# One encoder layer on one core: the scan's within-chunk products of a group run together, B-by-C products in pairs, transposes may be held back longer

## The chip, the core and the metric

The kernel runs on one core of a Trainium2 chip. The metric is the device time of one execution in microseconds (us); of the kernel before it is 1085.19 us, the median of 3 runs from 1084.91 to 1087.61. The engines are TensorE (PE in the profile; its weight loads are PEld), VectorE (DVE), ScalarE (ACT), GpSimd (POOL) and SyncE (SP, which issues the DMAs).

## The reference

One layer of a bidirectional hybrid encoder: 512 tokens, 1024 channels, everything float32.

```python
h = rmsnorm(x, pre_mix_norm)
z, xbc, dt_raw, q, k, v, gates = split_cols(h @ w_in, IN_SPLITS)     # 1024 x 10816
y_ssd  = ssd_branch(z, xbc, dt_raw, ...)                             # 32 heads of 64, 8 groups, state 128, chunk 128
y_attn = window_attention(q, k, v, sink, rel_table) @ w_attn_out     # 16 heads, 4 kv heads, +-128 tokens
g = sigmoid(gates + b_gate)
x = x + rmsnorm((g_ssd * y_ssd + g_attn * y_attn) @ w_o, post_mix_norm)
x = x + rmsnorm(square(relu(rmsnorm(x, pre_mlp_norm) @ w_mlp_in)) @ w_mlp_out, post_mlp_norm)
```

The change lies in `ssd_branch`, whose core is a scan in chunks of 128 tokens, run once forward and once on the flipped sequence, the two results added:

```python
cb = einsum('bclgn,bcsgn->bcgls', c, b)                               # B by C in a chunk, one per group
y_diag = einsum('bcgls,bcgrls,bcsgrp->bclgrp', cb, decay, xdt)        # within a chunk
states = einsum('bclgn,bcgrl,bclgrp->bcgrpn', b, decay_states, xdt)
y_off = einsum('bclgn,bcgrpn,bcgrl->bclgrp', c, prev, exp(a_cs))      # from the chunks before
u = (y_fwd + y_bwd + xs * d_skip) * silu(z)
u = u * rsqrt(mean(u * u over the group) + EPS) * norm_w
```

## The kernel before

**Products.** The large products take both operands in two parts, a rounded one and the remainder (`wh` and `wl` for weights, `hi` and `lo` or names ending in `h` and `l` for activations), and sum three products of 512 columns per block of 128 inputs (`mm3`, through `mm` at L398). They are the *wide* products here. The weights come by DMA as `wr`, ScalarE rounds them to `wh` (L473), GpSimd or VectorE forms `wl` (L477), in rings of three buffers. The small products of scan and attention are plain float32 (`mm`), and so are transposes by the identity (`tr`, L402).

**The scan.** The input projection runs in quanta (one block of 128 output columns over all 512 tokens: 24 wide products). For each of 8 groups (4 heads, 256 channels) `ssd_steps` gives closures that are placed between quanta:

- `prep(c)`, once for each of the 4 chunks: B by C (two records on PE), masked for both directions on VectorE (`cb`, L1103), then `m`, the within-chunk weights of the 4 heads (L1104 to L1115).
- `states0`, `states1`: the state that enters each chunk (`pv`).
- `outs(j)`, once for each pair of chunks (1, 0) and (2, 3): `C` by `pv`, the four heads' products of `m` with `x`, then the sums: the state part times the decay `E` (L1143), the within-chunk part added to `w` (L1144, VectorE), `E` added (L1148, GpSimd), the gate `z` (L1149), squares (`sq`, ScalarE) and their sum `ssq` (L1156); after the second pair `ssq` is split in `sh` and `sl`.
- `rms`, `finish`: PE sums the squares over channels (`ps<-sh,ones_r` and `sl`), the root is taken by way of two DMAs, and the scaled result `yT` is kept and later split (`split_y`, L1233 and L1234). The output projection (`ssd_out_quanta`) uses the last two blocks, of group 7, in its step `rest`.

The products of `m` with `x` write 64 output partitions each and go in pairs to the two halves of the array's columns; so do the attention's products of `pT` with `V`. I call them *half-width*; each leaves two records in the profile, of 128 columns. A *stretch* is a run of half-width products with nothing else between; a *visit* is a run of anything small between wide products.

**What sets the order.** The code emits instructions in program order with its placements; `Planner` then orders each engine's instructions by itself, and the program is built in this order. The planner assigns each instruction a cost (`duration`) and PE a cost of changing between kinds (`change`); a *kind* is whether the operands are the rounded type, and whether the product is half-width. On PE, `next_matmul` takes the first ready instruction in program order, but stays with the present wide kind until another has been ready for `HOLD = 4000` ns; from a small kind it goes on with the same kind, then with any other small one. The other engines take the instruction that is due first. `depend` collects what each instruction waits for; `turn` says that an instruction may start only once another has started, for a buffer that is used in a ring.

## Time and profile before

| | |
|---|---|
| median of 3 runs | 1085.19 us (1084.91 to 1087.61) |
| the profiled execution | 1085.44 us |
| its span, first to last instruction | 1083.7 us |
| mean granted clock of TensorE | 0.997 |
| busy: PE, POOL, DVE, ACT | 1073.5, 808.1, 785.1, 654.4 us |

The span holds, in order: the start (to about 60 us), input projection, scan and attention (to about 619), the scan's output projection (to about 705), the mixing product and the MLP. The 8 groups' scans lie between about 118 and 640 us, a group every 53 us or so in the later part. A line of the timeline gives start, length, engine, source line, operation, output<-inputs by the program's names, shape and count; in brackets the idle time of the engine before it and what ended it. A line of the groups ends in count, busy us, mean ns, and idle time before.

### The profile page before, as it was taken

Reading aid. Unit: us, or ns where it says so; the run is one execution under the profiler, and the core shown is the slowest. Engines: PE = TensorE matmul, PEld = TensorE weight load, DVE = VectorE, ACT = ScalarE, POOL = GpSimd, SP = SyncE. Lnnn points to the kernel's source line nnn. Section 1 sums busy time; section 2 is a strip of 40 time slices with the busy share of each in tenths; the row PEclk is TensorE's granted clock in tenths of the full one; section 3 lists DMA queues with packets and bytes.
Section 4 is the critical chain, followed back from the end, with each engine's and each line's share of the span. In section 5 each row is a group of like instructions: output and inputs, shape, how many; then the busy total and the mean of one; then the engine's idle time right before and its main releaser. Section 6 shows DMA issues by size and latency. Waiting matters only on the chain.

```text
span 1083.7 us, 16956 instructions
## 1 busy us (share of the span) xinstructions
PE 1073.5 (99%) x5584; PEld 902.2 (83%) x5584; DVE 785.1 (72%) x1345; ACT 654.4 (60%) x1407; POOL 808.1 (75%) x1011
## 2 busy tenths in 40 slices
PE   9999999999999999999999999999999999999997
PEld 8888888888888888888888888889888888888885
DVE  6578787788796787887877558668873755755787
ACT  5566776686865767676686522476755434434443
POOL 4446567557558898989898768566998978978844
PEclk9999999999999999999999999999999999999999
DMA  7444624625536555556564389754722612611522
GB/s 218 118 121 125 150 76 123 146 74 158 131 107 164 149 144 160 158 143 167 136 179 113 103 253 332 226 198 127 237 65 59 201 53 59 198 55 59 161 93 78
DMA packets 221000, 152.21 MB, mean 140 GB/s; under 512 B 12493, under 2 KB 194229, under 8 KB 220912
## 3 DMA queue, kind: packets, MB, share of 16 engines
q1 hardware_dynamic: 220764, 151.06, 48.6%
q8 instruction: 44, 0.72, 0.3%
q14 instruction: 44, 0.36, 0.1%
q10 hardware_dynamic: 148, 0.07, 0.0%
HBM read 138.19 MB, written 12.91 MB: 139 GB/s over the span
## 4 chain that ended last, share of the span: by engine, by line
PE 94%; DVE 2%; DMA 2%; ACT 1%; SPq 1%; issue 1%; POOL 0%; POOLq 0%; DVEq 0%
PE pp L398 66%; PE ps L398 25%; PE ps L402 3%; DMA x<-in_x 1%; DMA wr<-in_w_in 0%; ACT b L423 0%; DVE B L944 0%; DVE x L1401 0%; DVE P L855 0%; DVE x L1655 0%; DVE acc L1621 0%; SPq L383 0%; SPq L570 0%; DVE Q L832 0%; DVE ag L1648 0%
## 5 line engine op out<-in xcount | busy, mean ns | idle before, releaser
L398 PE MATMUL pp<-b,wh 128*128 128x512 f32 (+1 forms) x1840 | 564.8, 388 | 0.2 <-DVE b L424 0.2
L477 POOL TENSOR_TENSOR wl<-wr,wh 128x256 fp32r<-128x256 f32 (+1 forms) x503 | 418.2, 860 | 137.4 <-ACT wh L473 133.9
L398 PEld LDWEIGHTS pp<-b,wh 128*128 128x128 f32 x1840 | 340.2, 188 | 68.2 <-issue 1.5
L398 PE MATMUL pp<-b,wl 128*128 128x512 f32 (+1 forms) x920 | 356.5, 388 | 0.0
L398 PEld LDWEIGHTS pp<-b,wl 128*128 128x128 f32 x920 | 172.9, 188 | 34.3
L473 ACT CAST wh<-wr 128x1024 fp32r<-128x1024 f32 x131 | 136.5, 1042 | 82.0 <-PE pp L398 56.1
L1575 POOL TENSOR_TENSOR wl<-wd,wh 128x256 fp32r<-128x256 f32 x168 | 139.8, 862 | 39.9 <-ACT wh L1571 31.9
L1571 ACT CAST wh<-wd 128x512 fp32r<-128x512 f32 x108 | 63.2, 618 | 53.9 <-PE pp L398 23.8
L398 PE MATMUL ps<-wh,fh 128*128 128x512 f32 (+1 forms) x196 | 75.5, 385 | 0.5 <-DVE acc L1621 0.5
L398 PE MATMUL ps<-wl,fh 128*128 128x512 f32 (+1 forms) x196 | 75.5, 385 | 0.0
L398 PE MATMUL ps<-wh,fl 128*128 128x512 f32 (+1 forms) x196 | 75.4, 385 | 0.0
L1112 ACT ACTIVATE n<-cb,tables 128x128 f32<-128x128 f32 x128 | 48.8, 391 | 26.8 <-DVE cb L1103 22.8
L1449 DVE SCALAR_TENSOR_TENSOR pp<-pp,r 128x512 f32<-128x512 f32 (+1 forms) x31 | 17.5, 565 | 54.0 <-ACT r L1446 53.9
L1575 POOL TENSOR_TENSOR wl<-wt,wh 128x256 fp32r<-128x256 f32 x56 | 45.4, 844 | 9.9 <-ACT wh L1571 6.0
L944 DVE SCALAR_TENSOR_TENSOR u<-pp,cv,u 128x510 f32<-128x510 f32 (+1 forms) x64 | 47.6, 744 | 2.9 <-ACT u L940 1.7
L1042 POOL TENSOR_TENSOR xd<-x,tables 128x256 f32<-128x256 f32 x48 | 35.0, 747 | 19.5 <-ACT x L967 16.9
L1113 ACT ACTIVATE m<-cb,tables 128x128 f32<-128x128 f32 x128 | 48.7, 389 | 0.3 <-DVE cb L1103 0.3
L1148 POOL TENSOR_TENSOR w<-w,E 128x256 f32<-128x256 f32 x48 | 40.3, 852 | 11.1 <-DVE w L1144 5.4
L398 PEld LDWEIGHTS ps<-wh,fh 128*128 128x128 f32 x196 | 36.8, 188 | 8.1 <-DVE acc L1621 0.7
L1108 ACT ACTIVATE rf<-rf,tables 128x128 f32<-128x128 f32 x128 | 41.9, 393 | 2.6 <-DMA rf<-csT 2.6
L398 PEld LDWEIGHTS ps<-wl,fh 128*128 128x128 f32 x196 | 36.8, 188 | 7.4
L398 PEld LDWEIGHTS ps<-wh,fl 128*128 128x128 f32 x196 | 36.8, 188 | 7.2
(301 smaller groups left out, 2085.3 us busy)
## 6 DMA issues: line engine op xcount, KB each, us to landing
wr<-in_w_in SPq DMA_DIRECT2D x74, 512.0 KB, 4.8
wr<-in_w_mlp_in SPq DMA_DIRECT2D x32, 512.0 KB, 4.1
wd<-in_w_mlp_out SPq DMA_DIRECT2D x64, 256.0 KB, 4.7
rb<-csT SPq DMA_DIRECT2D x32, 256.0 KB, 3.9
rf<-csT SPq DMA_DIRECT2D x32, 256.0 KB, 5.5
wr<-in_w_ssd_out SPq DMA_DIRECT2D x14, 512.0 KB, 5.4
wd<-in_w_o SPq DMA_DIRECT2D x28, 256.0 KB, 4.6
E<-csE SPq DMA_DIRECT2D x96, 64.0 KB, 3.9
```

Of the source, the lines that this page charges most:

```text
L398: self.nc.tensor.matmul(out, lhsT, rhs, start=start, stop=stop, skip_group_check=more)
L402: self.nc.tensor.transpose(out, src, self.ident[:n, :n])
L473: self.nc.scalar.copy(hi[:, :m], raw)
L477: engines[e].tensor_tensor(lo[:, c], raw[:, c], hi[:, c].bitcast(F32), op=ALU.subtract)
L944: nc.vector.scalar_tensor_tensor(u[:, a:e], ps[:, a + d:e + d], self.wtap(t, b), u[:, a:e], op0=ALU.mult, op1=ALU.add)
L1042: nc.gpsimd.tensor_tensor(v4(xd[:, d * 256:(d + 1) * 256]), v4(xs(c)), by_dir(self.coef, c)[:, d].unsqueeze(2).to_broadcast([128, 4, 64]), ...
L1108: nc.scalar.activation(v4(rf)[:, h], v4(rf)[:, h], AF.Identity, bias=ncs[:, 0, h:h + 1])
L1112: nc.scalar.activation(v4(n)[:, h], cb[:, 0], AF.Copy, scale=dt[:, 0, h:h + 1])
L1113: nc.scalar.activation(v4(m)[:, h], cb[:, 1], AF.Copy, scale=dt[:, 1, h:h + 1])
L1148: nc.gpsimd.tensor_tensor(wc, wc, E[:, d], op=ALU.add)
L1571: nc.scalar.copy(hi, w)
L1575: (nc.vector if e == "v" else nc.gpsimd).tensor_tensor(low[:, q], w[:, q], hi[:, q].bitcast(F32), op=ALU.subtract)
```

## The change

- `similar(j)` is new: the two chunks of a pair have their B-by-C products in one PSUM bank, masked by one VectorE operation of 512 columns. `prep` no longer has a product and reads its part.
- `outs` is cut in four: `cross(j)` (state part and its decay), `within(j)` (`m` with `x`, added to `w`), `total(j)` (`E` added) and `gated(j)` (gate, squares, sum). At the first place stand `cross(0)` and `total(0)`; at the second `cross(1)`, `within(0)`, `within(1)`, `gated(0)`, `total(1)`, `gated(1)`.
- In `next_matmul` a transpose that waits ends a wide run only after `2 * HOLD`, all else after `HOLD` as before.
- In `depend` every instruction that writes a ring buffer now has its turn after the first use of the buffer's predecessor; before, it was the first instruction that touches it.

```diff
--- before.py
+++ after.py
@@ -124,7 +124,8 @@
         if not kind[0]:
             other = [n for n in now if not self.kind[n][0]]
             return (same or other or now)[0]
-        return same[0] if same and min(ready[n] for n in now if self.kind[n] != kind) > t - self.HOLD else first
+        held = lambda n: ready[n] + (2 if self.ins[n].is_transpose else 1) * self.HOLD
+        return same[0] if same and min(held(n) for n in now if self.kind[n] != kind) > t else first
 
     @staticmethod
     def operands(aps):
@@ -155,7 +156,7 @@
 
     def depend(self):
         self.pre = [set() for _ in self.ins]
-        live, users, ring, seen, first, base = {}, {}, {}, {}, {}, {}
+        live, users, ring, seen, first, base, behind = {}, {}, {}, {}, {}, {}, {}
         self.turn = [set() for _ in self.ins]
         for n, i in enumerate(self.ins):
             for write, aps in ((False, i.ins), (True, i.outs)):
@@ -170,11 +171,13 @@
                             held = ring.setdefault(tag, [])
                             held.append(name)
                             if len(held) > 1:
-                                self.turn[n].add(first[held[-2]])
+                                behind[name] = first[held[-2]]
                             first[name] = n
                             if len(held) > bufs:
                                 base[name] = users[held[-1 - bufs]]
                                 live.pop(held[-1 - bufs])
+                    if write and name in behind:
+                        self.turn[n].add(behind[name])
                     key = (name, ap.offset, tuple(map(tuple, ap.ap)))
                     if key not in seen:
                         seen[key] = self.region(ap)
@@ -1093,14 +1096,21 @@
                         nc.sync.dma_start(ch[c]["E"][i * 64:(i + 1) * 64, d], src)
             return run
 
+        def similar(j):
+
+            pc, both = self.bank("ps"), get("cb", (128, 2, 2, 128))
+            st["cb"] = both
+            for u in range(2):
+                tok = slice((2 * j + u) * 128, (2 * j + u + 1) * 128)
+                self.mm(pc[:, u * 128:(u + 1) * 128], st["B"][:, tok], st["C"][:, tok], True, True)
+            products = pc[:, :256].rearrange("p (u t) -> p u t", u=2).unsqueeze(2)
+            nc.vector.tensor_tensor(both, products.to_broadcast([128, 2, 2, 128]),
+                                    self.UL.unsqueeze(1).to_broadcast([128, 2, 2, 128]), op=ALU.mult)
+
         def prep(c):
             def run():
-                tok = slice(c * 128, (c + 1) * 128)
                 rf, rb = ch[c]["r"]
-                pc = self.bank("ps")
-                self.mm(pc[:, :128], st["B"][:, tok], st["C"][:, tok], True, True)
-                cb = get("cb", (128, 2, 128))
-                nc.vector.tensor_tensor(cb, pc[:, :128].unsqueeze(1).to_broadcast([128, 2, 128]), self.UL, op=ALU.mult)
+                cb = st["cb"][:, c % 2]
                 cs, ncs, dt = by_dir(self.cs, c), by_dir(self.ncs, c), by_dir(self.dt, c)
                 m, n = get("m"), get("n")
                 nc.gpsimd.tensor_tensor(v4(rb), v4(rb), cs[:, 1].unsqueeze(2).to_broadcast([128, 4, 128]), op=ALU.subtract)
@@ -1113,15 +1123,16 @@
                     nc.scalar.activation(v4(m)[:, h], cb[:, 1], AF.Copy, scale=dt[:, 1, h:h + 1])
                 nc.vector.tensor_tensor(m, m, n, op=ALU.add)
                 nc.vector.tensor_tensor(m, m, rf, op=ALU.mult)
-                put(rf, rb, cb, n)
+                put(rf, rb, n)
+                if c in (0, 3):
+                    put(st["cb"])
                 ch[c]["m"] = m
             return run
 
-        def outs(j):
+        def cross(j):
 
             def run():
                 cs = (1, 0) if j == 0 else (2, 3)
-                w = st["w"][j]
                 yos = {}
                 for c in cs:
                     yo = yos[c] = self.bank("ps").rearrange("p (d i t) -> p d i t", d=2, i=2)
@@ -1129,6 +1140,17 @@
                         for i in range(2):
                             S = st["enter"][c][:, d * 256 + i * 128:d * 256 + (i + 1) * 128]
                             self.mm(yo[:, d, i], S, st["C"][:, c * 128:(c + 1) * 128], True, True)
+                for c in cs:
+                    dd = slice(dirs[3 - c][0], dirs[3 - c][-1] + 1)
+                    E = ch[c]["E"]
+                    nc.vector.tensor_tensor(E[:, dd], yos[c][:, dd], E[:, dd], op=ALU.mult)
+            return run
+
+        def within(j):
+
+            def run():
+                cs = (1, 0) if j == 0 else (2, 3)
+                w = st["w"][j]
                 yd = self.bank("ps").rearrange("p (c i t) -> p c i t", c=2, i=2)
                 for c in cs:
                     x, m = xs(c), ch[c]["m"]
@@ -1137,17 +1159,31 @@
                             h = 2 * i + u
                             self.mm(yd[u * 64:(u + 1) * 64, c % 2, i], x[:, h * 64:(h + 1) * 64], v4(m)[:, h], True, True)
                     put(m)
-                for c in cs:
-                    dd = slice(dirs[3 - c][0], dirs[3 - c][-1] + 1)
-                    E = ch[c]["E"]
-                    nc.vector.tensor_tensor(E[:, dd], yos[c][:, dd], E[:, dd], op=ALU.mult)
                 nc.vector.tensor_tensor(w, yd, w, op=ALU.add)
+
+            return run
+
+        def total(j):
+
+            def run():
+                cs = (1, 0) if j == 0 else (2, 3)
+                w = st["w"][j]
                 for c in cs:
                     wc, E = w[:, c % 2], ch[c]["E"]
                     for d in dirs[3 - c]:
                         nc.gpsimd.tensor_tensor(wc, wc, E[:, d], op=ALU.add)
+                    put(E)
+
+            return run
+
+        def gated(j):
+
+            def run():
+                cs = (1, 0) if j == 0 else (2, 3)
+                w = st["w"][j]
+                for c in cs:
+                    wc = w[:, c % 2]
                     nc.gpsimd.tensor_tensor(wc, wc, st["z"][j][:, c % 2], op=ALU.mult)
-                    put(E)
                 if "ssq" not in st:
                     st["ssq"] = get("ssq")
                 sq = get("sq", (128, 2, 2, 128))
@@ -1160,6 +1196,21 @@
                     hi, lo = st["sq"] = get("sh", dtype=F32R), get("sl", dtype=F32R)
                     self.split(hi, lo, st["ssq"])
                     put(st["ssq"])
+
+            return run
+
+        def outs(j):
+
+            def run():
+                cross(j)()
+                if j == 0:
+                    total(0)()
+                    return
+                within(0)()
+                within(1)()
+                gated(0)()
+                total(1)()
+                gated(1)()
             return run
 
         def rms():
@@ -1192,7 +1243,7 @@
             put(r, *st["w"])
             self.grp[g] = None
 
-        return weigh, states0, states1, [load(c) for c in range(4)], [prep(c) for c in range(4)], [outs(j) for j in range(2)], rms, finish
+        return similar, weigh, states0, states1, [load(c) for c in range(4)], [prep(c) for c in range(4)], [outs(j) for j in range(2)], rms, finish
 
     def place_head(self, h, q):
 
@@ -1206,12 +1257,14 @@
     def place_ssd(self, g, q):
 
         def place():
-            weigh, states0, states1, load, prep, outs, rms, finish = self.ssd_steps(g)
+            similar, weigh, states0, states1, load, prep, outs, rms, finish = self.ssd_steps(g)
             o = LAST if g == 7 else SCAN
             self.at(q(o["weigh"][0]), lambda: weigh((0, 3)))
             self.at(q(o["weigh"][1]), lambda: weigh((1, 2)))
             for i, c in enumerate(CHUNKS):
                 self.at(q(o["prep"][i] - o["load"]), load[c])
+            for j in range(2):
+                self.at(q(o["prep"][2 * j]), lambda j=j: similar(j))
             self.at(q(o["states"][0]), states0)
             self.at(q(o["states"][1]), states1)
             for i, c in enumerate(CHUNKS):
```

**PE in group 3 of the scan.** The names: `pv` entering states, `m` the within-chunk weights of one chunk (each row of them is one chunk's four heads), `u` the next group's channels, `ah`, `al`, `b` activations with `wh`, `wl`. Before, at three places of the group:

```order
L398 MATMUL ps_4467<-C_4076,pv_4285 128x128 x4
L398 MATMUL ps_4472<-C_4076,pv_4287 128x128 x2
L398 MATMUL ps_4475<-m_4302,x_3958 64x128 x4
L398 MATMUL pp_4382<-ah_3335,wh_4175 128x512
...
L398 MATMUL pp_4454<-b_168,wl_4255 128x512
L398 MATMUL ps_4475<-m_4406,x_3958 64x128 x4
L398 MATMUL ps_4526<-C_4076,B_3900 128x128
...
L398 MATMUL ps_4698<-C_4076,pv_4287 128x128 x2
L398 MATMUL ps_4701<-m_4530,x_3968 64x128 x4
L398 MATMUL ps_4701<-m_4602,x_3968 64x128 x4
L398 MATMUL pp_4680<-b_168,wh_4517 128x512
```

Now, at the two places that are left:

```order
L401 MATMUL ps_4446<-C_4058,pv_4272 128x128 x4
L401 MATMUL ps_4451<-C_4058,pv_4274 128x128 x2
L401 MATMUL ps_4489<-C_4058,B_3866 128x128 x2
L405 MATMUL ps_4611<-ident,u_4329 128x128
...
L401 MATMUL ps_4658<-C_4058,pv_4274 128x128 x2
L401 MATMUL ps_4663<-m_4285,x_3924 64x128 x4
L401 MATMUL ps_4663<-m_4385,x_3924 64x128 x4
L401 MATMUL ps_4673<-m_4494,x_3934 64x128 x4
L401 MATMUL ps_4673<-m_4562,x_3934 64x128 x4
L401 MATMUL pp_4640<-b_168,wh_4480 128x512
```

The three stretches of half-width products are one, at the place of the last; the first place keeps the state products and has the pair of B-by-C products. In the whole order of PE the half-width stretches are 29 before and 16 now, and the visits without one 36 before and 34 now.

**POOL at the end of group 7.** `w` with `E` and `z` are the sums and the gate of a half (the first half is w_6500 before and w_6442 now), `wl` are weight pieces. Before:

```order
L477 TENSOR_TENSOR wl_7074<-wr_6962,wh_7073 128x256
L1148 TENSOR_TENSOR w_6510<-w_6510,E_6721 128x256 x2
L1148 TENSOR_TENSOR w_6510<-w_6510,E_6815 128x256
L1149 TENSOR_TENSOR w_6510<-w_6510,z_6642 128x256 x2
L1156 TENSOR_TENSOR ssq_6937<-sq_6938 128x256
L1156 TENSOR_TENSOR ssq_6937<-sq_7120 128x256
L477 TENSOR_TENSOR wl_7074<-wr_6962,wh_7073 128x256
```

Now:

```order
L480 TENSOR_TENSOR wl_7010<-wr_6901,wh_7009 128x256
L1174 TENSOR_TENSOR w_6452<-w_6452,E_6679 128x256 x2
L1174 TENSOR_TENSOR w_6452<-w_6452,E_6774 128x256
L1186 TENSOR_TENSOR w_6442<-w_6442,z_6599 128x256 x2
L1186 TENSOR_TENSOR w_6452<-w_6452,z_6600 128x256 x2
L480 TENSOR_TENSOR wl_7010<-wr_6901,wh_7009 128x256
L1192 TENSOR_TENSOR ssq_7063<-sq_7064 128x256
L1192 TENSOR_TENSOR ssq_7063<-sq_7072 128x256
L480 TENSOR_TENSOR wl_7010<-wr_6901,wh_7009 128x256
```

The gate of the first half, two operations, and a weight piece stand between the second half's sums and the squares.

**PE where the output projection takes the last two blocks of the scan.** These are yh_7436 and yl_7437 before, yh_7388 and yl_7389 now; the other `yh`, `yl` are earlier blocks. Before:

```order
L398 MATMUL pp_7274<-yh_7436,wh_7321 128x512
L398 MATMUL pp_7349<-yh_7436,wh_7321 128x512
L398 MATMUL pp_7497<-yh_7225,wl_7393 128x512
L398 MATMUL pp_7497<-yh_7229,wh_7392 128x512
L398 MATMUL pp_7497<-yl_7230,wh_7392 128x512
L398 MATMUL pp_7497<-yh_7229,wl_7393 128x512
L398 MATMUL pp_7497<-yh_7233,wh_7392 128x512
L398 MATMUL pp_7497<-yl_7234,wh_7392 128x512
L398 MATMUL pp_7497<-yh_7233,wl_7393 128x512
L398 MATMUL pp_7274<-yl_7437,wh_7321 128x512
```

Now:

```order
L401 MATMUL pp_7226<-yh_7388,wh_7273 128x512
L401 MATMUL pp_7301<-yh_7388,wh_7273 128x512
L401 MATMUL pp_7449<-yh_7177,wl_7345 128x512
L401 MATMUL pp_7449<-yh_7181,wh_7344 128x512
L401 MATMUL pp_7226<-yl_7389,wh_7273 128x512
```

The first `yl` comes four products after the first `yh` instead of nine, so it is used five products earlier.

## The prediction

> **What bounds the kernel now.** I read the page first, for which engine fills the span and what the chain of work that ended last consists of:
>
> ```profile
> PE 1073.5 (99%) x5584; PEld 902.2 (83%) x5584; DVE 785.1 (72%) x1345; ACT 654.4 (60%) x1407; POOL 808.1 (75%) x1011
> PE 94%; DVE 2%; DMA 2%; ACT 1%; SPq 1%; issue 1%; POOL 0%; POOLq 0%; DVEq 0%
> ```
>
> TensorE (PE) is busy for 99% of the span and makes up 94% of the chain. A busy PE could still be one that often waits a little, so the view of waits, for PE alone, comes second (who waited for whom, total us, times, longest; one more row, of the start, is left out):
>
> ```profile
> PE ps L398 <- ACT b L415: 0.9, 1, 0.9
> PE ps L398 <- DVE acc L1621: 0.5, 1, 0.5
> PE pp L398 <- DVE b L424: 0.2, 1, 0.2
> ```
>
> Nothing of the scan stands there: no wait for `m`, `pv`, `u`, `wl` or `P`. The third view, busy time in stretches, shows how near the other engines are to becoming the bound; columns are PE, weight load, VectorE (DVE), ScalarE (ACT) and GpSimd (POOL), then the granted clock:
>
> ```profile
> 398.00:452.00 54.00, 54.00 (x288) 45.32 (x286) 42.78 (x63) 39.07 (x89) 49.09 (x61) 1.00 0.58 162
> ```
>
> This is one group of the scan: PE 54.0 of 54.0 us, POOL 49.1, the rest 43 or less, the clock at its full value. So in this stage only what shortens PE's own queue counts, and POOL has 9% to spare. Two rows give PE's steady pace, the first and the last column being start, length and count in the chain:
>
> ```profile
> 618.69 92.53 PE pp L398 x408
> 99.41 0.87 PE ps L402 x8
> ```
>
> A 512-column product takes 92.53/408 = 0.227 us, a transpose 0.87/8 = 0.109 us.
>
> **What a stretch of half-width products costs.** The within-chunk products (`m` with `x`) fill 64 columns of the array, as the attention's value products do; nearly everything else fills 128. The last two such stretches of group 7, in the timeline of PE (start, length, what; the length of one includes the pipeline, so I go from start to start):
>
> ```profile
> 587.85 0.39 PE L398 MATMUL pp<-b,wl 128*128 128x512 f32 x1
> 588.16 0.66 PE L398 MATMUL ps<-m,x 128*64 128x128 f32 x8
> 588.75 0.74 PE L398 MATMUL pp<-b,wh 128*128 128x512 f32 x2
> 589.33 0.40 PE L398 MATMUL pp<-b,wl 128*128 128x512 f32 x1
> ```
>
> ```profile
> 602.98 0.39 PE L398 MATMUL pp<-b,wl 128*128 128x512 f32 x1
> 603.30 1.09 PE L398 MATMUL ps<-m,x 128*64 128x128 f32 x16
> 604.32 0.73 PE L398 MATMUL pp<-b,wh 128*128 128x512 f32 x2
> 604.89 0.39 PE L398 MATMUL pp<-b,wl 128*128 128x512 f32 x1
> ```
>
> From the first row to the last are 1.48 us with 8 records (each product leaves two) and 1.91 us with 16, and three wide products in both. So 8 records cost 0.43 us, and what is left, 1.48 - 3 x 0.227 - 0.43 = 0.37 us, is the price of going into the half-width form and back, paid once per stretch however long it is. Where transposes follow, it is less:
>
> ```profile
> 478.13 0.39 PE L398 MATMUL pp<-b,wh 128*128 128x512 f32 x1
> 478.44 0.66 PE L398 MATMUL ps<-m,x 128*64 128x128 f32 x8
> 479.03 0.44 PE L402 MATMUL ps<-ident,u 128*128 128x128 f32 x2
> 479.23 0.48 PE L398 MATMUL pp<-b,wh 128*128 128x512 f32 x1
> 479.55 0.39 PE L398 MATMUL pp<-b,wl 128*128 128x512 f32 x1
> ```
>
> Here 1.42 - 2 x 0.227 - 0.43 - 2 x 0.109 = 0.32 us. In the full-width form, small FP32 products that cut into a wide product are nearly free:
>
> ```profile
> 570.03 0.38 PE L398 MATMUL ps<-C,B 128*128 128x128 f32 x2
> 570.17 0.48 PE L398 MATMUL pp<-b,wl 128*128 128x512 f32 x1
> 570.49 0.63 PE L398 MATMUL pp<-b,wh 128*128 128x512 f32 x2
> 570.96 0.40 PE L398 MATMUL pp<-b,wl 128*128 128x512 f32 x1
> ```
>
> 0.93 - 3 x 0.227 - 2 x 0.109 = 0.03 us. The bounds for one stretch are 0.32 and 0.40 (0.37 plus 0.03 for the wide product after it, which can start late too); I take 0.38, near the plain exits, which most stretches have.
>
> The Trainium skill ("TensorEngine Tiling (Array Packing)", Tiling Modes) says that a change of tiling mode drains TensorE, and "TensorE: Matmul & The Clock Gate" (Single matmul latency) puts a drain at about 175 ns. Two changes per stretch would be an estimate of 0.35 us, 4.6 us for the 13 stretches counted below; the trace's 0.37 is a little above it and decides.
>
> **The change, part by part.** *Fewer stretches.* Counted through the whole order of PE, the half-width stretches go from 29 to 16: the `m` products from 22 stretches to 9 (one per group but group 6, which keeps two), the 8 of attention stay, and one of each kind stand side by side before and after. 29 - 16 = 13; 13 x 0.38 = **4.9 us saved**, 4.2 to 5.2 by the bounds. The products themselves are as many as before.
>
> *Transposes held longer, B-by-C in pairs.* Visits of small products without a half-width stretch go from 36 to 34: 2 x 0.03 = 0.1 us. That the transposes may be held for twice as long therefore brings next to nothing by itself; it serves to put them beside the stretches.
>
> *The masking of B-by-C.* 32 operations of 256 columns become 16 of 512. VectorE's rows:
>
> ```profile
> L1103 DVE TENSOR_TENSOR cb<-ps,cst 128x256 f32<-128x256 f32 x32 | 13.1, 417 | 16.9 <-PE ps L398 16.7
> L1144 DVE TENSOR_TENSOR w<-ps,w 128x512 f32<-128x512 f32 x16 | 10.9, 682 | 3.6 <-PE ps L398 3.6
> ```
>
> 32 x 0.417 = 13.3 against 16 x 0.682 = 10.9 us, the second row being the nearest 512-column operation out of PSUM. VectorE gains 2.4 us, but it has 11 of 54 us free in a group, so this is worth 0 on the path; the first `m` of a pair starts 0.27 us later, ahead of products that now stand later for half of the chunks.
>
> *The end of a group.* The first half's gating and squares now wait until both halves' products are done. In the last group, where this chain is shortest of time, the rows of before are:
>
> ```profile
> 604.44 0.69 DVE L1144 TENSOR_TENSOR w<-ps,w 128x512 f32<-128x512 f32 x1 [2.23 <-PE ps L398]
> 611.01 2.92 DVE L416 TENSOR_TENSOR sl<-ssq,sh 128x512 fp32r<-128x512 f32 x1 [5.88 <-ACT sh L415]
> ```
>
> ```profile
> 605.21 2.23 POOL L1148 TENSOR_TENSOR w<-w,E 128x256 f32<-128x256 f32 x3 [0.32 <-DVE w L1144]
> 607.40 1.45 POOL L1149 TENSOR_TENSOR w<-w,z 128x256 f32<-128x256 f32 x2
> 608.80 1.52 POOL L1156 TENSOR_TENSOR ssq<-sq 128x256 f32<-128x256 f32 x2
> 610.28 3.11 POOL L477 TENSOR_TENSOR wl<-wr,wh 128x256 fp32r<-128x256 f32 x2
> ```
>
> ```profile
> 618.06 0.40 PE L398 MATMUL ps<-sh,ones_r 128*128 128x512 f32 x1
> ```
>
> `sl` is ready at 613.93 and PE reaches the sum over it at 618.06: 4.1 us of slack. The order of POOL now puts two more `w,z` (1.45 us) and one weight piece (about 0.7, taken as long as one `w,z`) between, 2.2 us, while PE's 16 extra records ahead of the sum move both ends by the same 0.86. The slack shrinks to about 1.9 us: cost 0 while that cover holds. If it went, PE would stand at the sum, and the output projection's weights behind it.
>
> *The last two blocks of the scan's output.* They are used five products earlier in PE's order than before; the rows of before:
>
> ```profile
> 639.22 2.21 DVE L1234 TENSOR_TENSOR yl<-yT,yh 128x512 fp32r<-128x512 f32 x2
> ```
>
> ```profile
> 641.47 0.39 PE L398 MATMUL pp<-yl,wh 128*128 128x512 f32 x1
> ```
>
> The first `yl` is done after half of 2.21, at 640.33; five products earlier, 641.47 - 5 x 0.227, is 640.33 as well. No slack is left, so I add 0.2 us of waiting, bounds 0 and 1.1 (one `yl`).
>
> **The sum.** The span of 1083.7 - 4.9 - 0.1 + 0.2 = 1078.9 us. The profiled execution took 1085.44, 1.7 more than its span; the median of the runs, 1085.19, is 1.5 more. So I predict 1078.9 + 1.5 = **1080.4 us**, 0.4% faster.
>
> **The rivals.** *Waiting at the joined stretches (no change that can be told).* A joined stretch and the work shifted around it could find an operand late: `m` of the last chunk, a `P` behind a held transpose, `yl`. Against it: PE waited for none of these before, and the joined stretch stands where the second of the two stood. For it: the order was made with durations that are not those of the trace, and 9 joined stretches need only wait 0.2 us each, plus 1.1 at `yl`, for 4.8 - 1.8 - 0.9 = 2.1 us to be left: **1083.1**. Below 3.3 us (0.3%) a gain can't be told from none in a measurement of this kernel.
>
> *POOL becomes the bound (slower).* In each group three operations of POOL, two `w,z` and one `ssq`, 1.45 + 0.76 = 2.2 us, move from the middle of the group into the burst behind its last products, where weight pieces for PE queue behind them. If PE then has to wait for the pieces by that much, 8 x 2.2 = 17.6 us are lost and the time is 1080.4 + 17.6 = **1098.0**; it decides once pieces are ready less than 2.2 us ahead of their use, and from half of it (8.1 us lost) the change is slower than before. What speaks for it is POOL's 49.1 of 54 us; against it speak the waits:
>
> ```profile
> POOL wl L477 <- ACT wh L473: 133.9, 68, 8.2
> ACT wh L473 <- PE pp L398: 56.1, 23, 4.8
> ```
>
> POOL sat idle for 133.9 us before weight pieces because ScalarE had not rounded the weights, and that because PE still held the buffer. POOL runs a buffer ahead of PE, not behind it.
>
> A rule of the Trainium skill speaks for this rival: by "SBUF — State Buffer" (SBUF: two separate sides) VectorE with two SBUF inputs and GpSimd exclude each other for a whole instruction. The trace agrees in one place: `sl`, 2.92 us above beside POOL's 3.11, where 512 columns take 0.69 in `w`. By that rule a denser burst of POOL would stretch `sl` by up to 2.2 us more, which is the 1.9 us of slack gone and 0.3 us lost; 8 x 0.3 = 2.4 us and 1082.8 if all eight groups had as little slack as the last. I give this 0.04, out of the 0.18 for waiting below.
>
> *A dearer stretch.* If each of the 13 saves 0.40 and `yl` is in time, it is 1083.7 - 5.2 - 0.1 + 1.5 = **1079.9**. It differs from the forecast by size alone and belongs to its range.
>
> **How the numbers follow.** Forecast, with the dearer stretch: 0.74. Waiting that eats a third or more of the gain, so that less than 0.3% is left: 0.18. POOL or another engine as the bound, slower by more than 0.3%: 0.08. That gives 0.74 faster, 0.18 same, 0.08 slower. The likeliest case alone lies between 1079 and 1082; the range of 8 in 10 starts at 1078.8, a little under the dear stretch, and reaches up over the waiting rival to 1085.2.
>
> **What would show it.** In the changed kernel's timeline of PE: `m,x` in rows of 32 records beside each other in seven of the eight groups, and the same 0.37 us around each. In the view of waits for PE: no row for `wl`, `m` or `sl`, at most about 1 us for `yl`. POOL's busy time unchanged within 1%, VectorE's about 2 us less, and the whole gain before 640 us of the span, with the stage after it as long as before. The prediction is wrong if PE shows waits of more than 2 us in the scan, if the price of a stretch grows with its length, or if the joined stretch is preceded by wide products that start late.

## The result: about 0.4% faster, 3.9 us off the span, with 0.8 us lost at one place that the prediction didn't name

The changed kernel takes 1081.49 us in the median (five runs, 1081.3 to 1081.95), against 1085.19 for the kernel before (five runs, 1084.91 to 1089.14): 3.7 us or 0.34% less. The measured ratio is 0.9955, 95% interval 0.9937 to 0.9973; it agrees with the ratio of the means, into which the two longest runs of before (1087.61 and 1089.14) enter. 1080.4 had been predicted. The span goes from 1083.7 to 1079.8 us, and the profiled execution took 1081.6. The page of the changed kernel, busy time of the engines and shares of the chain that ended last:

```profile
PE 1069.0 (99%) x5584; PEld 901.8 (84%) x5584; DVE 788.5 (73%) x1329; ACT 656.0 (61%) x1407; POOL 807.0 (75%) x1011
PE 94%; DVE 3%; ACT 1%; issue 1%; DMA 1%; POOL 0%; POOLq 0%; DVEq 0%; ACTq 0%
```

PE has as many instructions as before and 4.5 us less busy time: they are the same products, less often interrupted. But the span fell by 3.9 only, and VectorE's part in the chain rose from 2 to 3%. The view of waits, for PE, shows two new rows, the second and the third here (three rows that both kernels have are left out):

```profile
PE ps L401 <- ACT b L418: 0.9, 1, 0.9
PE pp L401 <- DVE b L1287: 0.5, 1, 0.5
PE ps L401 <- DVE pT L884: 0.3, 1, 0.3
```

The first row, of the start, is as long as before. To see which stage gave what, I cut both spans at the same wide products in PE's order: numbers 224 (where the scan's part begins), 2304 and 2390 of 4380, counted from 0. Busy time in these stretches (columns: PE, weight load, VectorE, ScalarE, GpSimd, granted clock, DMA share, GB/s), before:

```profile
61.40:618.50 557.10, 557.02 (x3165) 468.38 (x3164) 430.96 (x775) 393.56 (x921) 424.59 (x524) 1.00 0.51 136
618.50:638.10 19.60, 19.60 (x88) 16.19 (x87) 7.72 (x10) 6.95 (x11) 10.56 (x9) 1.00 0.57 174
638.10:1083.70 445.60, 437.40 (x2023) 365.78 (x2021) 309.75 (x483) 219.90 (x407) 346.00 (x434) 1.00 0.45 142
```

And after:

```profile
61.50:613.90 552.40, 552.09 (x3166) 468.10 (x3165) 429.39 (x754) 395.08 (x921) 424.44 (x524) 1.00 0.51 136
613.90:634.20 20.30, 19.83 (x88) 16.07 (x87) 11.70 (x14) 6.90 (x11) 10.60 (x10) 1.00 0.65 193
634.20:1079.80 445.60, 437.46 (x2023) 365.68 (x2021) 310.06 (x482) 219.83 (x407) 344.98 (x434) 0.99 0.45 142
```

The scan stage is 4.7 us shorter, the stage behind it 0.7 us longer, and the rest is as it was. (The cuts are rounded to 0.1 us here; from the starts of the products themselves the scan is 4.71 shorter and the next stage, called the *tail* below, 0.77 longer.) In the tail VectorE has 4.0 us more of busy time, in the scan 1.6 less.

**The scan stage** is what the count of stretches says. A joined stretch in group 5, in PE's timeline:

```profile
486.53 0.39 PE L401 MATMUL pp<-b,wl 128*128 128x512 f32 x1
486.77 0.81 PE L405 MATMUL ps<-ident,u 128*128 128x128 f32 x6
487.42 1.50 PE L401 MATMUL ps<-C,pv 128*128 128x128 f32 x12
488.85 1.97 PE L401 MATMUL ps<-m,x 128*64 128x128 f32 x32
490.75 0.73 PE L401 MATMUL pp<-b,wh 128*128 128x512 f32 x2
491.32 0.39 PE L401 MATMUL pp<-b,wl 128*128 128x512 f32 x1
```

All 32 records stand together. From the first row to the last are 4.79 us; less three wide products (0.68), 18 small ones at 0.109 (1.96) and 32 records at 0.43/8 (1.72), 0.43 are left, of which 0.03 belong to the visit as such. So about 0.40 us. The 0.37 for 8 and for 16 records were worked out from those two stretches together, so this third length is the first test: the price hardly grows, by 0.03 us for four times the records.

**The tail** is where the gain leaks. The chain of waits there (start, length, what):

```profile
608.81 0.63 ACT sh L418
609.47 2.92 DVE sl L419
612.39 2.87 DVE yl L1287 x2
615.26 1.51 DVE b L1287 x3
616.77 2.42 issue
619.19 4.14 DVE b L1287 x4
623.38 16.65 PE pp L401 x72
```

These are the splits of group 7's squares (`sl`) and of earlier blocks of the scan's output (`yl`, `b`) on VectorE. They run back to back, each behind the one before, until PE waits for the last `b`. The 2.42 us of "issue" are not idle time: in VectorE's own rows (number, then shortest, median and longest duration in ns) one `b` takes all of it, and it lies beside one weight piece of GpSimd:

```profile
L1287 DVE TENSOR_TENSOR b<-yT,b x8: 676/680/2882, 615.2 to 623.2; 128x512 fp32r<-128x512 f32 x8
```

```profile
616.38 2.88 DVE L1287 TENSOR_TENSOR b<-yT,b 128x512 fp32r<-128x512 f32 x1
```

```profile
616.25 2.47 POOL L480 TENSOR_TENSOR wl<-wr,wh 128x1024 fp32r<-128x1024 f32 x1 [2.14 <-ACT wh L476]
```

The `b` starts 0.13 us after the piece and ends 0.54 us after it, as if it had waited out GpSimd's whole instruction and then done most of its usual 0.68 us. Three more of the row are stretched in the same way: `sl` (2.92 us) and the first `yl` (2.34) end 0.55 and 0.54 us after a piece of GpSimd, and so does the `b` that PE waits for:

```profile
621.00 2.33 DVE L1287 TENSOR_TENSOR b<-yT,b 128x512 fp32r<-128x512 f32 x1
```

```profile
620.73 2.05 POOL L480 TENSOR_TENSOR wl<-wr,wh 128x768 fp32r<-128x768 f32 x1
```

PE, at the sum over the squares and at the end of the row of splits:

```profile
613.40 0.39 PE L401 MATMUL ps<-sh,ones_r 128*128 128x512 f32 x1
...
622.51 0.39 PE L401 MATMUL pp<-yl,wh 128*128 128x512 f32 x1
623.38 0.50 PE L401 MATMUL pp<-b,wh 128*128 128x512 f32 x1 [0.47 <-DVE b L1287]
```

The sum did not wait, `sl` was ready at 612.39. At the end there are 0.87 us from start to start in place of 0.23, and the product after it comes 0.1 late as well: that is 0.74 of the 0.77. The kernel before had a stretched `b` too, but an idle engine ahead of it:

```profile
L1234 DVE TENSOR_TENSOR b<-yT,b 128x512 fp32r<-128x512 f32 x8 | 7.0, 910 | 3.6 <-ACT b L1233 3.6
```

There the eight `b` took 7.0 us with 3.6 us of idle time between them (waiting for ScalarE); after, they take 8.7 with none.

### The profile page after: what moved, and what is told of

It reads as the page before. It is cut to its first block, busy times and chain, and to the rows that moved or that the text cites. A ratio compares the mean times of both kernels' runs of the same rounds, so it can differ in the third digit from the quotient of the medians.

```text
span 1079.8 us, 16931 instructions
## 1 busy us (share of the span) xinstructions
PE 1069.0 (99%) x5584; PEld 901.8 (84%) x5584; DVE 788.5 (73%) x1329; ACT 656.0 (61%) x1407; POOL 807.0 (75%) x1011
## 4 chain that ended last, share of the span: by engine, by line
PE 94%; DVE 3%; ACT 1%; issue 1%; DMA 1%; POOL 0%; POOLq 0%; DVEq 0%; ACTq 0%
PE pp L401 66%; PE ps L401 26%; PE ps L405 3%; DMA wr<-in_w_in 1%; DVE b L1287 1%; ACT b L426 0%; DVE sl L419 0%; DVE yl L1287 0%; DVE b L419 0%; DVE wv L584 0%; DVE junk L622 0%; DVE x L1454 0%; DVE x L1708 0%; ACT wh L476 0%; DVE acc L1674 0%
## 5 line engine op out<-in xcount | busy, mean ns | idle before, releaser
L867 ACT ACTIVATE P<-P,mx 128x384 f32<-128x384 f32 (+1 forms) x64 | 35.3, 555 | 11.6 <-DVE mx L864 11.6
```

What stands on the lines that cost most here:

```text
L867: nc.scalar.activation(p[:, :w], p[:, :w], AF.Exp, bias=mx[:, n:n + 1], accum_out=sm[:, n:n + 1])
```

## The experiments

The theory: the time goes with the number of half-width stretches, 0.38 us each, and the tail loses 0.77 us because the chain `sl`, `yl`, `b` on VectorE starts late. Rivals: the gain comes from holding transposes or from fewer and larger B-by-C masks; the loss in the tail is the use of `yl` five products earlier, or lies in `sl` alone. All runs first, each ratio against runs of the kernel before on the same chip (medians of before there: 1085.11 us for e1 to e4, 1085.36 for e5 to e8, 1085.30 for e9 to e11); a ratio need not be the quotient of two medians; "scan" and "tail" are the differences of the two stages to before in us, cut as above; "waits" are PE's waits for operands in the scan, from the view of waits (idle time alone). Of e6's -4.79 us, 0.23 are the product that it leaves out.

| kernel | stretches | median us (runs) | ratio, 95% | scan | waits | tail |
|---|---|---|---|---|---|---|
| before | 29 | 1085.19 (5) | 1 | 0 | 0 | 0 |
| the change | 16 | 1081.49 (5) | 0.9955, 0.9937 to 0.9973 | -4.71 | 0.3 | +0.77 |
| e1 pairs and hold, not joined | 24 | 1083.73 (11) | 0.9989, 0.9980 to 0.9998 | -1.57 | 0.3 | 0 |
| e2 four stretches per group | 35 | 1090.27 (5) | 1.0045, 1.0032 to 1.0059 | +6.46 | 4.2 | 0 |
| e3 joined alone | 19 | 1085.15 (11) | 1.0000, 0.9991 to 1.0009 | -1.01 | 2.0 | 0 |
| e4 hold as before | 16 | 1080.94 (5) | 0.9962, 0.9950 to 0.9975 | -5.13 | 0 | +0.79 |
| e5 last group apart | 17 | 1080.76 (5) | 0.9958, 0.9945 to 0.9972 | -4.38 | 0.3 | 0 |
| e6 no remainder of squares | 16 | 1080.69 (5) | 0.9958, 0.9945 to 0.9970 | -4.79 | 0.3 | 0 |
| e7 three `b` on GpSimd | 16 | 1081.10 (5) | 0.9962, 0.9949 to 0.9974 | -4.74 | 0.3 | +0.49 |
| e8 e7, hold as before | 16 | 1081.02 (5) | 0.9960, 0.9948 to 0.9973 | -5.12 | 0 | +0.48 |
| e9 the change again | 16 | 1081.14 (5) | 0.9960, 0.9949 to 0.9972 | -4.75 | 0.3 | +0.76 |
| e10 e5, hold as before | 17 | 1080.93 (5) | 0.9955, 0.9943 to 0.9967 | -4.74 | 0 | 0 |
| e11 sums over states early | 16 | 1081.23 (6) | 0.9960, 0.9948 to 0.9973 | -4.38 | 0 | 0 |

### What the stretches cost: e1, e2, e3, e4

**e1** keeps the pairs and the longer hold, but runs the `m,x` products in two places, as before:

```diff
                 cross(j)()
-                if j == 0:
-                    total(0)()
-                    return
-                within(0)()
-                within(1)()
-                gated(0)()
-                total(1)()
-                gated(1)()
+                within(j)()
+                total(j)()
+                gated(j)()
```

> The change without its joining: each half of a group keeps its own place for the within-chunk products, its sums and its gate; B-by-C pairs, one mask and the longer hold of transposes stay. Counted in PE's order, half-width stretches are 24 (29 before, 16 in the change). Theory (each stretch costs 0.38 us whatever its length, nothing else counts): 5 x 0.38 = 1.9 us faster than before, ratio 0.998, and no wait at the split of the scan's blocks (`b`), since the first half's gate is early again. Rival (the gain of the change comes from the pairs and the hold, not from the count of stretches): as fast as the change, 0.996. Rival (the gain is all in the joining): same as before, 1.000.

24 stretches are left: in every group but one, the two chunks of a half now run together (17 stretches of `m` in place of 22). Scan -1.57, and with the wait for `pT` (the attention's transposed weights) taken out -1.87: 5 x 0.374. In the median it is 1.4 us faster than before, and the interval excludes both rivals, 1.000 only just.

**e2** goes the other way: one stretch per chunk, placed 1.5 quanta apart.

```diff
...
             def run():
                 cross(j)()
-                if j == 0:
...
+                within(j, 0)()
+            return run
+
+        def outs2(j):
+
+            def run():
+                within(j, 1)()
+                total(j)()
+                gated(j)()
             return run
...
+                self.at(q(o["outs"][j] + GAP), outs[j + 2])
```

> The change with the within-chunk products taken apart the other way: each of a group's four chunks has its own place, PSUM bank and add. The products are the same; half-width stretches are 35 (16 in the change, 29 before). Sixteen more additions of 256 columns on VectorE, off PE's path. Theory: 19 x 0.38 = 7.2 us slower than the change, 6 x 0.38 = 2.3 us slower than before, ratio to before 1.002. Rival (a stretch costs less where it is short, the price is in its products): within 0.5 us of the change, 0.996.

It lost more than twice as much as the count says, also in the median (5.2 us; the profiled execution is the slowest of the five, 1.2 us above it). PE's waits in this kernel, three rows left out as above, show the rest:

```profile
PE ps L402 <- ACT pT L885: 2.7, 2, 2.5
PE ps L402 <- DVE C L955: 0.9, 1, 0.9
PE ps L402 <- ACT b L419: 0.5, 1, 0.5
PE ps L406 <- DVE P L874: 0.3, 1, 0.3
PE ps L402 <- DVE pT L885: 0.3, 1, 0.3
```

Without the row of the start (`b`) these are 4.2 us; 6.46 - 4.2 = 2.26 for six stretches more, 0.377 each. They are waits for operands; that the other order makes these late is argued, not shown.

**e3** joins the stretches, with B-by-C in each chunk's `prep` and the hold as they were before:

```diff
-        held = lambda n: ready[n] + (2 if self.ins[n].is_transpose else 1) * self.HOLD
+        held = lambda n: ready[n] + (1 if self.ins[n].is_transpose else 1) * self.HOLD
...
-                cb = st["cb"][:, c % 2]
+                tok = slice(c * 128, (c + 1) * 128)
+                pc = self.bank("ps")
+                self.mm(pc[:, :128], st["B"][:, tok], st["C"][:, tok], True, True)
+                cb = get("cb", (128, 2, 128))
+                nc.vector.tensor_tensor(cb, pc[:, :128].unsqueeze(1).to_broadcast([128, 2, 128]), self.UL, op=ALU.mult)
...
```

> The joining alone: B by C one chunk at a time with its own mask as before, and transposes held no longer than the rest. Half-width stretches are 19. Theory: 10 x 0.38 = 3.8 us faster than before less the 0.8 us that the change waits at the split of the last blocks, ratio 0.9972, and three stretches (1.1 us) slower than the change. Rival (the joining alone carries the gain): as fast as the change, 0.9955 or below.

This one missed: no gain at all in the median of eleven runs, which scatter from 1083.96 to 1087.16. The profiled execution, 1084.02, is the second fastest of them, so the profile shows a gain that most runs don't have. In it PE waits for `pT` as nowhere in the kernel before:

```profile
PE ps L401 <- ACT pT L884: 1.7, 1, 1.7
PE ps L401 <- DVE pT L884: 0.3, 1, 0.3
```

These 2.0 us and the 1.01 gained make 3.0 for ten stretches, 0.30 each, 0.8 us short of the rule. Most of the 0.8 us lies beside the same waits, whose rows hold only PE's idle time. Counted from start to start, the products that come late with no change of form just before them lose 2.78 us in e3 and 0.10 in the kernel before; with that taken out 3.69 us are gained, 0.37 each. Counted so, the change has 0.67 us (0.41 per stretch), e4 none (0.39), e1 0.95 (0.48) and e2 5.51 (0.18): where ten stretches or more are saved the price holds, but the agreement of e1 and e2 above hangs on how a wait is counted. Why e3's runs scatter more than the others' stays open.

**e4** is the change with the hold of before:

```diff
-        held = lambda n: ready[n] + (2 if self.ins[n].is_transpose else 1) * self.HOLD
+        held = lambda n: ready[n] + (1 if self.ins[n].is_transpose else 1) * self.HOLD
```

> The change with the hold of transposes set back to that of all other products. Half-width stretches stay 16, visits of other small products are 39 instead of 34. Theory: 5 x 0.03 = 0.15 us slower than the change, not to be told from it, ratio 0.9957. Rival (the held transposes carry part of the gain): slower than the change by 0.5 us or more, 0.996 or above. Rival (the longer hold costs by late transposes): faster than the change, 0.995 or below.

The same 16 stretches, no wait for `pT`, scan -5.13 (13 x 0.395). Holding transposes for longer brings nothing here; in the profiles it costs the 0.3 us at `pT`, a row that is gone in e8, e10 and e11 as well, which also hold as before. In the medians this can't be told from zero.

Beside e3, e4 says more: the two kernels differ in the pairs alone. Without pairs the scan is 1.01 us shorter than before, with them 5.13, and the medians are 1085.15 and 1080.94. So the pairs are what makes the joining pay: with them three more stretches go, and the waits for `pT` as well. Whether that comes of PE's order or of the earlier masks is not separated.

### Where the tail loses: e5, e6, e7

**e5** leaves group 7, whose end is short of time, as it was: its first half finishes at its own place.

```diff
                 cross(j)()
+                if g == 7:
+                    within(j)()
+                    total(j)()
+                    gated(j)()
+                    return
                 if j == 0:
```

> The change, but in group 7, the last, each half keeps its own place for products, sums and gate. 17 half-width stretches. In the change PE lost 0.77 us at 622.5 to 623.4 us to `b`, the split of the scan's blocks on VectorE, which came late behind `sl` (2.92 us) and two `yl`. Theory (the joined last group's burst on GpSimd holds up VectorE there): the wait is gone and one stretch more is paid, 0.77 - 0.38 = 0.4 us faster than the change in the span, 1079.4, and no wait for `b`. Rival (VectorE is late there for work that has nothing to do with the joining): the wait stays, 0.4 us slower, 1080.2.

The tail is as long as before and PE has no wait for `b`. VectorE's timeline shows the chain earlier:

```profile
607.34 1.89 DVE L1292 TENSOR_TENSOR yl<-yT,yh 128x512 fp32r<-128x512 f32 x2 [2.50 <-ACT yh L1291]
609.37 1.01 DVE L419 TENSOR_TENSOR sl<-ssq,sh 128x512 fp32r<-128x512 f32 x1
611.58 9.71 DVE L1292 TENSOR_TENSOR b<-yT,b 128x512 fp32r<-128x512 f32 x8 [1.20 <-ACT b L1291]
```

Over scan and tail it is 0.44 us ahead of the change (-4.38 against -3.94), as expected. Both `yl` are done ahead of `sl`, `sl` takes 1.01 in place of 2.92 us, and the eight `b` begin at 611.58, 3.6 us earlier than in the change (615.18). They take even longer there, 9.71 us; one is stretched to 2.89 beside the same 1024-column piece of GpSimd. The stretching is thus not new, and costs nothing as long as the row begins early enough.

**e6** takes one link out: group 7's squares go to PE unsplit, rounded (`sl` and its product are left out there).

```diff
-                    self.split(hi, lo, st["ssq"])
+                    if g == 7:
+                        nc.scalar.copy(hi, st["ssq"])
+                        put(lo)
+                        st["sq"] = hi,
+                    else:
+                        self.split(hi, lo, st["ssq"])
...
```

> The change, but group 7's sum over squares takes the rounded part alone: the remainder `sl` is neither formed on VectorE (2.92 us in the change) nor multiplied (one wide product of 0.23 us less on PE). That part of the computation is left out. Theory (`sl`, held up by GpSimd, is what makes `b` late): 0.77 + 0.23 = 1.0 us faster than the change, span 1078.8, no wait for `b`. Rival (`yl` and `b` themselves are too slow beside GpSimd): 0.23 us faster, 1079.6, and a wait for `b` of 0.3 us or more.

Tail 0 as well, with the stretches still joined, and over scan and tail 0.85 us ahead of the change where 1.0 had been expected:

```profile
610.60 2.21 DVE L1292 TENSOR_TENSOR yl<-yT,yh 128x512 fp32r<-128x512 f32 x2 [4.55 <-ACT yh L1291]
612.73 10.95 DVE L1292 TENSOR_TENSOR b<-yT,b 128x512 fp32r<-128x512 f32 x8
```

The `b` begin 2.4 us earlier and are done early enough, though they take 10.95 us. So the loss hangs on when the row of splits begins. It is not the use of the last blocks' `yl` five products earlier: that lies behind this stage, at 636.45 us in the change, and PE has no wait there.

**e7** gives three of the eight `b` to GpSimd:

```diff
-            nc.vector.tensor_tensor(lo, self.yT[k], hi.bitcast(F32), op=ALU.subtract)
+            (nc.gpsimd if k in (7, 10, 13) else nc.vector).tensor_tensor(lo, self.yT[k], hi.bitcast(F32), op=ALU.subtract)
```

> The change, but three of the sixteen remainders of the scan's output blocks are formed on GpSimd, which stands idle for over 2 us near 614 us in the change, and not on VectorE. Theory (VectorE has too much to do between 609 and 624 us): three times 0.7 to 1.5 us less there, the wait of 0.77 us gone, span 1079.0. Rival (the two engines exclude each other, so the work takes as long wherever it is): same as the change within 0.2 us, span 1079.8.

The tail loses 0.49 in place of 0.77 us. The chain of waits now goes through GpSimd:

```profile
611.66 1.37 POOL b L1287
613.02 0.77 POOL wl L480
613.79 1.46 issue
615.25 1.76 POOL b L1287
617.00 2.82 POOL wl L480
```

The work that was moved queues with the weight pieces, and PE stands behind a piece instead of a `b`. The span, 1079.0 us, is the one that the theory named, but by luck: 0.5 us of it are a shorter start (61.01 in place of 61.50 us to the first cut), and over scan and tail e7 is only 0.3 us ahead of the change.

### Put together: e8, e9, e10, e11

**e8** is e7 with e4's edit.

```diff
-        held = lambda n: ready[n] + (2 if self.ins[n].is_transpose else 1) * self.HOLD
+        held = lambda n: ready[n] + (1 if self.ins[n].is_transpose else 1) * self.HOLD
...
+            (nc.gpsimd if k in (7, 10, 13) else nc.vector).tensor_tensor(lo, self.yT[k], hi.bitcast(F32), op=ALU.subtract)
```

> The run before this one, with the hold of transposes set back to that of all other products as well; 16 half-width stretches. That hold alone gave a span of 1078.7 against 1079.8 of the change, with the wait for `b` still in it. Theory (both are independent): 1078.7 - 0.8 = 1077.9 in the span, ratio to before about 0.9950, faster than the change by 0.1 to 0.2%. Rival (the 1.1 us were the scatter of where small waits fall): 1079.0, as the run before this one.

**e9** is the change itself, with no edit, beside e7 and e8 on one chip.

> The change itself, once more, on one chip with the two runs after it, which it is to be compared with: 0.9955 of before, span 1079.8 up to what the start of the program scatters by (the first wide weights were in use between 60.8 and 62.2 us in the profiles so far, whatever the kernel).

**e10** is e5 with e4's edit.

```diff
-        held = lambda n: ready[n] + (2 if self.ins[n].is_transpose else 1) * self.HOLD
+        held = lambda n: ready[n] + (1 if self.ins[n].is_transpose else 1) * self.HOLD
...
+                if g == 7:
+                    within(j)()
...
```

> Both parts that cost the change something taken away: group 7 not joined (17 half-width stretches) and transposes held no longer than the rest. Theory (both independent): no wait for `b` (0.77 us back), one stretch more (0.38), and the 0.4 us that the runs with the shorter hold were ahead in the scan: 0.8 us faster than the change, ratio to the change 0.9993, to before 0.9950. Rival (the shorter hold has no effect of its own): 0.4 us faster.

**e11** takes `cross` and `total` of both halves at the first place, a quantum later, so that less is left for GpSimd at the end of every group; the hold is that of before.

```diff
-... outs=(2.5, 5.5), rms=9, ...
+... outs=(3.5, 5.5), rms=9, ...
...
-                cross(j)()
                 if j == 0:
-                    total(0)()
+                    for k in range(2):
+                        cross(k)()
+                        total(k)()
                     return
                 within(0)()
                 within(1)()
                 gated(0)()
-                total(1)()
                 gated(1)()
```

> The change with the shorter hold, and both halves' state products and sums (`cross` and `total`) at the first of the two places, moved from 2.5 to 3.5 quanta, so that only the within-chunk products, gate and squares are left at the second. Half-width stretches stay 16, two of `yl` stand ahead of `sl` in VectorE's order again. Theory (the burst on GpSimd behind the joined products is what makes `b` late): 2.2 us less of it, no wait for `b` in the tail, 0.77 + 0.4 = 1.2 us faster than the change, ratio to before 0.9945. Rival (more state products at one place wait for their states or banks): a wait of PE for `pv` or `E` in the scan, no faster than the change.

All four agree with the parts: scan -4.4 to -5.1, tail 0 where the row of splits begins early (e10, e11), 0.5 where three blocks are on GpSimd (e8). Over both stages e8, e10 and e11 are 0.7, 0.8 and 0.4 us ahead of the change, where 1.9, 0.8 and 1.2 had been expected. In the medians none stands clear of the change: from 1080.69 to 1081.49 for all kernels with 16 or 17 stretches, with intervals of the ratio that overlap nearly whole. The 0.8 us of the tail can be taken back in the profile, but as a faster kernel none of these versions is shown.

e11's scan gained 0.75 us less than e4's. Its view of waits has no row of PE there, for `pv` and `E` neither. But two weight loads of the attention's products stood still for `pT`, behind a wide product that was still running:

```profile
158.03 0.19 PEld L401 LDWEIGHTS ps<-KH,Q 128*128 128x128 f32 x1 [0.53 <-ACT pT L884]
158.70 0.19 PEld L401 LDWEIGHTS ps<-KH,Q 128*128 128x128 f32 x1 [0.37 <-DVE pT L884]
```

From start to start, these two products and the two behind them come 0.68 us late in sum, where e4 has nothing of the kind.

## Why the prediction was right, point by point

- **Price of a stretch, 0.38 us (bounds 0.32 to 0.40), by 13.** Right in the size and in the rule. The scan stage without its 0.3 us wait is 5.0 us shorter, 0.385 per stretch. Counts of 16, 17, 24 and 35 give 0.37 to 0.395 once the waits that the profile shows are taken out; only e3 (0.30) and e11 (0.34) fall short. With what stands beside the waits counted too, e3 and e11 come to 0.37 and 0.38 and the change to 0.41, but e1 to 0.48 and e2 to 0.18, so over few stretches the price is less sure than these figures look. The lengths of 8 and 16 could not test that it is independent of length, as 0.37 came from both together; the 0.40 at 32 did.
- **The visits and the longer hold, 0.1 us.** Right for the hold as far as it can be seen: without it the time is the same (e4). For the pairs it says too little. They were priced by the visits alone, but without them three of the 13 stretches stay and the median shows no gain (e3 beside e4). The sum is not touched, since all 13 stretches were counted for the change as a whole.
- **The masking, 0 on the path, 2.4 us of VectorE.** Right: the 16 wide masks take 11.0 us after, 10.9 had been worked out, and no wait of PE follows from them.

```profile
L1107 DVE TENSOR_TENSOR cb<-ps,cst 128x512 f32<-128x512 f32 x16 | 11.0, 686 | 7.2 <-PE ps L401 7.0
```

- **The end of a group, "cost 0 while that cover holds".** This step failed. What it looked at held: `sl` was ready at 612.39 and PE reached the sum at 613.40, 1.0 us of slack where 1.9 were worked out, and no wait. But it followed the chain into PE only, and did not ask what stands behind `sl` on VectorE itself: the two `yl` and the eight `b`, which start 3.6 us later than they would without the joined end of group 7 (e5). That cost 0.77 us and was priced at nothing.
- **The last two blocks, +0.2 us.** Not there: the first `yl` is ready at 636.14 and used at 636.45, so 0.3 us of slack are left (the number, then shortest, median and longest duration of the two, and PE's row):

```profile
L1287 DVE TENSOR_TENSOR yl<-yT,yh x2: 808/1017/1226, 635.3 to 636.1; 128x512 fp32r<-128x512 f32 x2
```

```profile
636.45 0.40 PE L401 MATMUL pp<-yl,wh 128*128 128x512 f32 x1
```

  So 0.2 us were put at the wrong place, and 0.77 were lost at another: the sum of 1078.9 for the span was 0.9 short of 1079.8, of which 0.57 are this and 0.3 the wait for `pT`. Another 0.2 us of the 1.1 between 1080.4 and 1081.49 come from the step from span to median, 1.7 us where 1.5 were taken.
- **The rival of waiting.** It came true in a small part: 1.1 us in all, not at the joined stretches. **POOL as the bound** did not: no row for `wl` among the change's waits, and GpSimd's busy time is 0.1% less. (The 8.1 us from which the change was to be slower are the gain of 4.8 and the 3.3 below which nothing was to be told; 4.8 alone would undo the gain.)
- **VectorE about 2 us less.** Wrong for the whole span (3.4 us more), right for the scan stage (1.6 less); the 4.0 more in the tail are partly work that moved there, partly stretched operations, and 1.0 more lies in the start and behind the tail.
- **The rule on VectorE and GpSimd** of the Trainium skill ("SBUF — State Buffer", SBUF: two separate sides), that VectorE with two SBUF inputs and GpSimd reading SBUF exclude each other for a whole instruction, had been weighed for `sl`, at up to 2.2 us more. `sl` took 2.92 us before and after. By that rule a `b` beside the 2.47 us piece must wait it out; the trace agrees, with 2.88 us where 0.68 is usual. `sl`, one `yl` and another `b` of the row are stretched likewise. The mechanism was right, its place was not.

## What to carry to other kernels

Where one engine is busy for 99% of the span, count how often it changes its form and price one change from two runs of different length in its timeline: here that gave 4.9 us where 4.7 to 5.0 came. When a chain of work is moved later, follow it not only to the engine that bounds the kernel but also along its own engine's queue, to everything that stands behind it, and ask whether that still has an idle gap ahead of it; one here had 3.6 us of such gaps and lost all of them. Moving part of a late row to the neighbour engine brought 0.3 of the 0.8 us here, since it queued there with the weight pieces (e7). And a part of a change that seems to carry no gain can be what the rest needs: take it out alone before calling it small (e3 beside e4).

## What was not expected

- The start of the program scatters by as much as the versions differ: PE's one wait for `b` there was 0.9 us in the first profile of the change and 1.4 in the second (e9), and from 0.2 (e7) to 2.4 us (e11) in the others. In e11, whose runs lie from 1079.85 to 1083.96 us, the profiled start is 2.8 us longer than that of before. Spans of single profiles can thus not be compared below a microsecond or two unless the stages are.
- One operation of VectorE took 2.88 us in place of 0.68, and three near it 2.3 to 2.9, without a single waiting row: the chain calls part of the time "issue", and VectorE counts as busy. Busy time that grows with the same work was the only sign of it.
